# Output projection: the first head group's product stays in SBUF, and the list of steps counts transfers by size

## The chip, the cores and the metric

One Trainium2 chip, one core of it. The metric is the device time of one execution in microseconds (us); the time of a kernel is the median of its runs. A core has five engines that work at the same time, each through its own instructions in order: TensorE (PE, matrix products; PEld is its loading of weights), VectorE (DVE), ScalarE (ACT), GpSimd (POOL), and SyncE (SP), which here issues nearly all transfers between DRAM and the on-chip memory SBUF. Transfers run on 16 DMA engines. Products land in PSUM, in eight banks. An engine that waits for a semaphore holds up everything behind it in its order.

## The reference

One layer of a streaming encoder, float32, 1024 positions of 1024 features:

```
proj = rmsnorm(x) @ w_in                 # q, k, v of two head groups, and forget gates
y_fox = forgetting_attention(...)        # 8 heads of 64, causal
y_chk = chunked_relpos_attention(...)    # 8 heads of 64, a band of 9 chunks of 64
y = concat([rmsnorm(y_fox) * g_fox_out, rmsnorm(y_chk) * g_chk_out])     # 1024 x 1024
x = x + rmsnorm(y @ w_out) * g_mix_post          # the output projection
x = x + rmsnorm(memory_cross_attention(rmsnorm(x), rmsnorm(mem))) * g_mem_post
x = x + rmsnorm(square(relu(rmsnorm(x) @ w_ff1)) @ w_ff2) * g_ff_post
```

As y has two halves with an inverse root of their own per position, y @ w_out is the product of group 0 (fox) scaled by its root, plus that of group 1 (chk) scaled by its root.

## The kernel before

Every float32 product is made of three products of a rounded part (hi) and the rest (lo): `mm3` emits hi x hi (L174), lo x hi (L175) and hi x lo (L176). A weight block of 512 KB is loaded by SP (`wraw...`, L321), rounded on ACT (L338, `whi`), and its rest is formed on DVE (L343) or POOL (L346), `wlo`.

**The list of steps.** The order of the instructions of a large part of the kernel is not written out; it is made while the program is built, by a small simulation (`Flow`). Streams of PE steps each have a condition and an assumed duration; at each point of the list's own clock the first stream whose condition holds gives its next step. Other work is put into one line per engine: "V" (DVE), "S" (ACT), "G" (POOL) and "D" (transfers on SP), with an assumed cost and a level (the lower one goes first). What a step waits for is `there(key)`: the key has an assumed time, and it is past. The list decides order only; on the chip each engine waits for what it really needs. `flow.load` puts a transfer: 0.55 on line "D", then `took` until it counts as landed (4.5 unless given). Only one transfer stands on line "D" at a time.

Room is counted as tokens: `free["u4"]` for the 31 tiles of 128 x 1024 float32 that most of the layer shares (tag `u4`), `free["raw"]` for the 3 buffers of raw weight blocks, `free["mm"]` for 2 PSUM banks, `free["klo"]` for 4 tiles of attention keys, and so on.

**The stretch around the change** (phase 1 of the list, after the attention's projections; PE between about 480 and 660 us):

1. `fold_steps`: the memory keys are multiplied into w_mq, so that logits come from one product. There are two halves (k = 0, 1), each over four blocks `mq`; a block gives two banks, which ACT copies out (L944, tile `fm`). A finished tile of 512 KB is stored (`ml`, L920). When the four stores of a half have landed, POOL forms four sums (L913), which are stored too (`mlT`, L909), each after a delay of 10.0 times its number on the list's clock.
2. `mix_steps(0)`: group 0's products `yw`, in the order (th, nh) = (0,0), (0,1), (1,0), (1,1), where th is a half of the positions and nh a half of the output features, four row blocks each, 12 matrix products of 128 x 512 for each of the 16. They need `parts[th, 0]`, prepared by `Outputs`: it reads four transposed head outputs of 256 KB from DRAM (`oin` from `od`, L1072), which ACT scales and rounds (`yT_hi`, L1066) and DVE completes (`yT_lo`, L1067); ACT squares them (L1069), DVE adds the squares (`sq`, L1047), PE transposes them (`ssh`, L1096, `rstd_steps`), and DVE and POOL make the inverse root `rs`. `Outputs` goes through (th, g) = (0,0), (1,0), (0,1), (1,1), and takes seven `u4` tiles for one.
3. ACT copies a finished product, scaled by `rs`, to a tile `yt` of tag `klo` (L1233); SP stores it to DRAM (`yd`, L1235).
4. `memory_value_steps`: memory values from w_mv (`mv`).
5. `Back` loads group 0's rows from `yd` again into four `u4` tiles `yw` per half (L1206), and `mix_steps(1)` adds group 1's products to them on DVE (L1244). That is phase 2 of the list.

`Stock` loads the weight blocks ahead of use in one fixed order (mq, then wo of group 0, mv, wo of group 1, ml, mo); the dma is emitted at once, and line "D" only counts its time. wo and mv may go to a free `u4` tile when the three raw buffers are taken (`SPARE`), if 12 are free. What a split block occupies, its home, is a pair of tags `w`, `wq` or two `u4` tiles.

Of the kernel before, what the change touches and what calls it, by code (L numbers as in the profile page):

```python
# [22 lines left out]
P = 128  # L23
# [11 lines left out]
def f(ap):  # L35
    return ap.bitcast(F32)
# [19 lines left out]
class Flow:  # L56
# [15 lines left out]
        self.count += 1  # L72
        self.waiting[eng].append((level, at, self.count, cost, call, then))

    def load(self, at, call, then=None, took=4.5):
        self.put("D", at, 0.55, call, then and (lambda end: then(end + took)))

    def chain(self, at, parts, then=None, level=2):

# [56 lines left out]
def build(ctx, tc, nc, out, t):  # L136
# [65 lines left out]
    rall = const.tile([P, TB], F32, name="rall")  # L202

    od = [[dr.tile([3, P, HT], F32, name=f"od{k}_{h}") for h in range(2)] for k in range(KC)]
    yd = [dr.tile([P, D], F32, name=f"yd{b}") for b in range(TB)]
    x1d = [dr.tile([P, D], F32, name=f"x1d{b}") for b in range(TB)]
    x2d = [dr.tile([P, D], F32, name=f"x2d{b}") for b in range(TB)]
    rd = dr.tile([8, 768], F32, name="rd")
# [61 lines left out]
    class Stock:  # L270
# [3 lines left out]
        def __init__(self):  # L274
            self.blocks = []
            for n, (kind, pr) in enumerate(ORDER):
                if n == 5:
                    self.blocks.append("norm")
                b = (0 if kind == "f" else 8) + pr
                self.blocks.append((("q", n), t["w_qk"][b], [P, KC, P]))  # L280
                if n > 3:
                    self.blocks.append((("v", n), t["w_v"][n - 4], [P, KC, P]))
                if n == 7:
                    self.blocks.append("mem")
                self.blocks.append((("k", n), t["w_qk"][b + 4], [P, KC, P]))
            self.blocks += [(("mk", nb), t["w_mk"][nb], [P, KC, P]) for nb in range(KC)]
            self.blocks += [(("mq", kc), t["w_mq"][kc], [P, KC, P]) for kc in FOLD]
            pair = [P, 2, HT]
            self.blocks += [(("wo", 0, nh, i), row_pair(t["w_out"], i, nh), pair) for nh in range(2) for i in range(2)]
            self.blocks += [(("mv", nh, kp), row_pair(t["w_mv"], kp, nh), [P, 2, HT])  # L290
                            for nh in range(2) for kp in range(4)]
            self.blocks += [(("wo", 1, nh, i), row_pair(t["w_out"], 2 + i, nh), pair) for nh in range(2) for i in range(2)]
            ml = [[(("ml", 0, pr, kp), mld[pr][kp], pair) for pr in range(2) for kp in range(4)],
                  [(("ml", 1, p, k), src(k), pair) for p, (_, src) in enumerate(ML) for k in range(2)]]
            self.blocks += ml[0] + ml[1]
            self.blocks += [(("mo", 0, p, kp), src(kp), pair) for p, (_, src) in enumerate(MO) for kp in range(2)]
            self.blocks += [(("mo", 1, nh, kp), row_pair(t["w_mo"], kp, nh), pair)
                            for nh in range(2) for kp in range(4)]
            self.home = {("q", 0): "u4", ("k", 0): "u4", ("wo", 0, 1, 0): "u4", ("wo", 0, 1, 1): "u4", ("wo", 1, 1, 0): "wq", ("wo", 1, 1, 1): "u4"}
            self.home.update({(w, nb): "u4" for nb in range(1, KC, 2) for w in ("mk", "mq")})  # L300
            self.home.update({("mv", nh, kp): "u4" for nh in range(2) for kp in (1, 3)})
            self.home.update({("mo", 1, 0, kp): "wq" for kp in (1, 3)})
            turn = 0
            for b in self.blocks:
                if b[0][0] in ("ml", "mo"):
                    if b[0][:3] == ("mo", 1, 1):
                        self.home[b[0]] = "u4"
                    elif b[0][:2] == ("ml", 1) and b[0][3] == 1:
                        self.home[b[0]] = "u4"
                    elif b[0][:2] != ("mo", 1):  # L310
                        self.home[b[0]] = ("w", "wq")[turn % 2]
                        turn += 1
            self.raw, self.w, self.turned, self.spare = {}, {}, 0, {}
            self.to_load, self.to_split = list(self.blocks), []
# [50 lines left out]
        def pump(self):  # L365

            while self.to_load:
# [13 lines left out]
                    break  # L381
                free["u4" if self.spare[key] else "raw"].take()
                self.load()
                flow.put("D", flow.now, 0.55, lambda: None, lambda at, k=key: seen.__setitem__(("raw", k), at + 4.2))
            while self.to_split and there(("raw", self.to_split[0])):
                key = self.to_split[0]
                home = self.home.get(key, "w")
# [505 lines left out]
    def fold_steps(keep):  # L893
        km = keep.pop(0)
        stored, sums = all_of("folded", 8), all_of("summed_up", 8)
        for k in range(2):
            raw = {}

            def after(at, k=k, raw=raw):
                T = {"T1": (0, 0), "T3": (0, 1), "T2": (1, 1), "T4": (1, 0)}  # L900
                steps = [("T1", (0, 1), (0, 0)), ("T3", (1, 1), (0, 1)), ("T2", (1, 1), (0, 0)), ("T4", (1, 0), (1, 1))]

                def go(at, i=0):
                    if i < 4:
                        n, x, y = steps[i]
                        d = raw[T[n]]

                        def summed(end, n=n, d=d, i=i):
                            flow.load(end + 10.0 * i, lambda: nc.sync.dma_start(mlt[n][k], d),  # L909
                                      lambda e: (free["u4"].give(e), sums(e)), 3.0)  # L910
                            go(end, i + 1)

                        flow.put("G", at, 2.4, lambda: nc.gpsimd.tensor_sub(d, raw[x], raw[y]), summed, 1)  # L913

                go(at)
# [2 lines left out]

            def split(at, a, pr, k=k, raw=raw, summing=summing):
                flow.load(at, lambda: nc.sync.dma_start(mld[pr][a * 2 + k], raw[a, pr]),  # L920
                          lambda e: (stored(e), summing(e)), 3.0)

            for a in range(2):
                part = {}
# [2 lines left out]
                for j in range(2):  # L927
                    kc = a * 4 + k * 2 + j
                    for pr in range(2):
                        for h in range(2):  # L930
# [14 lines left out]
                            d, ps.rearrange("p a b -> p (a b)"), AF.Copy, scale=gm[:, kc:kc + 1]),  # L945
                            lambda at, bk=bk, one=part[pr]: (free[bk].give(at), one(at)), 1)
                    stock.done(("mq", kc))
        for _ in range(4):
            free["u4"].give(flow.end)

# [71 lines left out]
    class Outputs:  # L1022
# [5 lines left out]
        def pump(self):  # L1028
            while self.left:
                th, g = self.left[0]  # L1030
                if not (there(("od", g, th)) and ((th, g) == (0, 0) or there("keys")) and free["u4"].ready(13 if (th, g) == (0, 0) else 9)):
                    break
                self.left.pop(0)
                for _ in range(7):
# [3 lines left out]
        def one(self, th, g):  # L1038
# [19 lines left out]
            for i in range(2):  # L1058
                for j in range(2):
# [9 lines left out]
                            lambda end: (split(end), flow.put("S", end, 0.63, lambda: nc.scalar.activation(  # L1069
                                dst, o, AF.Square), squared, 1)), 1)  # L1070

                    flow.load(flow.now, lambda o=o, src=od[kc][th]: nc.sync.dma_start(o, src[0]), loaded, 5.0)  # L1072

    outputs = Outputs()
    waiting = {}
# [55 lines left out]
    class Rows:  # L1131
# [5 lines left out]
        def pump(self):  # L1137
            while self.left and free["xt"].ready() and stock.past("wo"):
# [7 lines left out]
                    xin[nm, n] = p2.tile([P, D], F32, tag="xt", bufs=2, name=f"xt{nm}{n}")  # L1146
                    nc.sync.dma_start(xin[nm, n], t["x"][n * P:(n + 1) * P, :] if nm == "w" else x1d[n])

                flow.load(flow.now, load, mark(("xt", nm, n)))

    def close_row(nm, n, at, dst, gnext, then):

# [10 lines left out]

        def store(end):
            free["xt"].give(end)
            flow.load(end, lambda: nc.sync.dma_start(dst[n], y), mark(("x1d", n)) if nm == "w" else None, 3)

            def inverse():
                c = r2[:, n:n + 1]
# [18 lines left out]
        nc.gpsimd.tensor_scalar(e, s2, EPS, EPS ** 0.5, op0=ALU.add, op1=ALU.mult)  # L1188
        nc.gpsimd.tensor_tensor(e, e, e, op=ALU.mult)

    stored = [all_of(("yd", th), 8) for th in range(2)]

    class Back:


        def __init__(self):
            self.left = [0, 1]

        def pump(self):
            while self.left and there(("yd", self.left[0])) and free["u4"].ready(6) and (  # L1200
                    there(("rs", 1, 1)) if self.left[0] else there("vm")):
                th = self.left.pop(0)
                y_tiles("w", th)
                done = all_of(("yb", th), 4)
                for b in range(4):
                    flow.load(flow.now, lambda b=b, th=th: nc.sync.dma_start(ys["w", th][0][b], yd[th * 4 + b]), done)  # L1206

    def y_half(name):
        return p1.tile([P, HT], F32R, tag="klo", bufs=4, name=name)

    def mix_steps(g):

        for th, nh in ((0, 0), (0, 1), (1, 0), (1, 1)):
            cs = slice(nh * HT, (nh + 1) * HT)
            for b in range(4):
                c = slice(b * P, (b + 1) * P)
                for k in range(4):
                    yield (0.681, lambda: k % 2 or there(("wo", g, nh, k // 2)) and (k or
                           there(("y", th, g)) and free["mm"].ready()
                           and (free["klo"].ready() if g == 0 else there(("yb", th)))))  # L1220
                    if k == 0:
                        free["mm"].take()
                        if g == 0:
                            free["klo"].take()
                        ps = mm_tile([P, HT], f"yw{th}{g}{nh}{b}")
                        yh, yl, sq = parts[th, g]
                    wh, wl = stock.w["wo", g, nh, k // 2]
                    mm3(ps, yh[k // 2][:, k % 2, c], yl[k // 2][:, k % 2, c],
                        wh[:, k % 2, :], wl[:, k % 2, :], k == 0, k == 3)
                if g == 0:  # L1230
                    yt = y_half(f"yt{th}{nh}{b}")
                    def leave(at, yt=yt, ps=ps, th=th, b=b, cs=cs):
                        flow.put("S", at, 0.63, lambda: nc.scalar.activation(  # L1233
                            f(yt), ps, AF.Copy, scale=parts["rs", th, 0][:, b:b + 1]), lambda at: (
                                free["mm"].give(at), flow.load(at, lambda: nc.sync.dma_start(yd[th * 4 + b][:, cs], f(yt)),  # L1235
                                                               lambda end: (free["klo"].give(end), stored[th](end)), 2.3)))

                    when(("rs", th, 0), flow.end, leave)
                else:
# [537 lines left out]
    def filler_steps(keep):  # L1777
# [9 lines left out]
        seen["paired"] = flow.end  # L1787
        yield from memory_key_steps(keep)
        yield from fold_steps(keep)
        seen["keys"] = flow.end  # L1790
        yield from mix_steps(0)
        yield from memory_value_steps(keep)

    def attention_phase():
# [3 lines left out]
            for th in range(2):  # L1798
                seen["v", n, th] = 0.0
        biases = Biases()  # L1800
        flow.pumps += [stock.pump, biases.pump, outputs.pump, back.pump, WeightSums().pump]
        flow.run([value_steps(), turn_steps(), score_steps(), side_steps(), rstd_steps(0), rstd_steps(1, (0,)),
                  filler_steps(keep)])
        return keep

    stock = Stock()
    back = Back()
    with tc.manual_schedule():
        nc.scalar.dma_start(gp, t["g_pre"])
        tiny = small.tile([P, 1], F32, tag="tiny", bufs=1, name="tiny")  # L1810
# [872 lines left out]
```

## Time and profile before

| what | us |
|---|---|
| median of 3 runs (1461.63 to 1462.76) | 1462.01 |
| the profiled execution | 1461.79 |
| its span, first to last instruction | 1460.0 |
| PE busy in the span | 1440.4 |
| DVE busy | 967.8 |
| ACT busy | 848.7 |
| POOL busy | 438.4 |

The kernel moves 274.13 MB, 188 GB/s over the span; the mean granted clock of TensorE was 0.997. Busy time of PE counts matrix products whose ends overlap, so 99% busy is not 99% of its peak. In rows of the profile "a<-b" is a tile written from a tile read, in the kernel's names with buffer numbers left out; `x12` is a count; what stands in square brackets behind an instruction is how long its engine had been idle, and what released it. A row of a window gives its length, the busy time of PE, PEld, DVE, ACT and POOL with their counts, the granted clock, the DMA engines' share and GB/s.

### The profile page before, as it was taken

To read this page: it belongs to the slowest core of one execution; us is meant where nothing else is said; L and a number is where in the kernel's file an instruction comes from. 1 tells how busy PE (TensorE), PEld (TensorE's weight loads), DVE (VectorE), ACT (ScalarE), POOL (GpSimd) and SP (SyncE) were. 2 spreads that over 40 slices of the span, in tenths; PEclk is the share of its full clock that TensorE was granted. 3 is DMA by queue.
4 is the path that set the end of the run, shared out by engine and by line. 5 is a ranking of instruction groups with operands and counts; after the bars stand their busy time and mean duration, and the time that the engine had idled before them with its cause. 6 is when DMAs were issued, how large, how long until landed. Compare 5 with 4: busy or idle time off the path is not lost.

```text
span 1460.0 us, 21001 instructions
## 1 busy us (share of the span) xinstructions
PE 1440.4 (99%) x7212; PEld 1216.8 (83%) x7212; DVE 967.8 (66%) x1661; ACT 848.7 (58%) x1510; POOL 438.4 (30%) x493
## 2 busy tenths in 40 slices
PE   9999999999999979999999999999999999999998
PEld 9888888888889968888788878888888888888886
DVE  5577778867677455786776587765555656655576
ACT  7457776667577745567886465545555443444442
POOL 1345555445344460252302504343322000000021
PEclk9999999999999999999999999999999999999999
DMA  8234567854546898573345557754444785445565
GB/s 333 69 98 97 143 168 185 279 125 114 130 103 189 267 326 297 204 240 102 108 152 196 188 165 244 256 199 159 159 146 164 287 318 182 136 149 196 182 251 202
DMA packets 105291, 274.13 MB, mean 188 GB/s; under 512 B 13257, under 2 KB 25809, under 8 KB 105185
## 3 DMA queue, kind: packets, MB, share of 16 engines
q1 hardware_dynamic: 100432, 264.40, 54.1%
q0 software_dynamic: 4608, 8.39, 3.8%
q8 instruction: 57, 0.93, 0.3%
q14 instruction: 50, 0.40, 0.1%
q10 hardware_dynamic: 144, 0.00, 0.0%
HBM read 188.28 MB, written 84.47 MB: 187 GB/s over the span
## 4 chain that ended last, share of the span: by engine, by line
PE 91%; DVE 3%; DMA 3%; ACT 2%; issue 1%; POOL 0%; DVEq 0%; POOLq 0%; SPq 0%; ACTq 0%
PE pv L654 4%; PE fx L175 4%; PE fx L176 4%; PE fx L174 4%; PE ptr L604 4%; PE fy L175 3%; PE fy L176 3%; PE fy L174 3%; PE px L176 3%; PE px L174 3%; PE px L175 3%; PE k L174 2%; PE k L176 2%; PE k L175 2%; PE q L174 2%; PE pz L174 2%
## 5 line engine op out<-in xcount | busy, mean ns | idle before, releaser
L610 DVE TENSOR_TENSOR p<-ptr,p 128x512 fp32r<-128x512 f32 (+1 forms) x152 | 92.3, 616 | 31.6 <-ACT p L613 30.4
L2405 ACT ACTIVATE whif<-ra 128x1024 fp32r<-128x1024 f32 x37 | 39.3, 1061 | 127.0 <-PE fy L175 62.6
L2519 POOL TENSOR_SCALAR rf<-sf,e 128x1 f32<-128x1 f32 x8 | 8.5, 1068 | 324.2 <-ACT jf L2504 324.2
L2407 DVE TENSOR_TENSOR wlof<-ra,whif 128x1024 fp32r<-128x1024 f32 x37 | 45.3, 1225 | 89.4 <-ACT whif L2405 89.4
L613 ACT ACTIVATE p<-ptr 128x512 fp32r<-128x512 f32 (+1 forms) x152 | 79.6, 538 | 42.7 <-PE ptr L604 41.9
L654 PE MATMUL pv<-p,vs 128*128 128x512 f32 (+1 forms) x304 | 86.2, 371 | 0.4 <-DVE p L610 0.4
L176 PE MATMUL fx<-vhif,wlof 128*128 128x512 f32 x168 | 65.4, 389 | 0.0
L174 PE MATMUL fx<-vhif,whif 128*128 128x512 f32 x168 | 65.4, 389 | 0.0
L175 PE MATMUL fx<-vlof,whif 128*128 128x512 f32 x168 | 65.4, 389 | 0.0
L2294 POOL TENSOR_TENSOR sc<-wf,wf 128x512 f32<-128x512 f32 x14 | 22.2, 1583 | 141.9 <-DMA wf<-in_w_ff 116.0
L654 PEld LDWEIGHTS pv<-p,vs 128*128 128x128 f32 x304 | 53.1, 189 | 8.8 <-DVE p L610 0.8
L174 PE MATMUL yw<-whiwo,yT_hi 128*128 128x512 f32 x128 | 51.2, 400 | 5.5 <-ACT yt L1233 5.5
L174 PE MATMUL k<-hT_hi,whik 128*128 128x512 f32 x128 | 52.6, 411 | 0.0
L175 PE MATMUL yw<-wlowo,yT_hi 128*128 128x512 f32 x128 | 50.7, 396 | 1.0 <-DVE wlowo L343 1.0
L174 PE MATMUL q<-hT_hi,whiq 128*128 128x512 f32 x128 | 51.0, 399 | 0.0
L176 PE MATMUL yw<-whiwo,yT_lo 128*128 128x512 f32 x128 | 50.5, 395 | 0.0
L176 PE MATMUL k<-hT_hi,wlok 128*128 128x512 f32 x128 | 50.2, 392 | 0.0
L175 PE MATMUL k<-hT_lo,whik 128*128 128x512 f32 x128 | 50.2, 392 | 0.0
L175 PE MATMUL q<-hT_lo,whiq 128*128 128x512 f32 x128 | 50.1, 391 | 0.0
L176 PE MATMUL q<-hT_hi,wloq 128*128 128x512 f32 x128 | 50.0, 391 | 0.0
L174 PE MATMUL fy<-vhif,whif 128*128 128x512 f32 x128 | 49.8, 389 | 0.0
L175 PE MATMUL fy<-vlof,whif 128*128 128x512 f32 x128 | 49.8, 389 | 0.0
(747 smaller groups left out, 5013.2 us busy)
## 6 DMA issues: line engine op xcount, KB each, us to landing
ra<-gd SPq DMA_DIRECT2D x56, 512.0 KB, 3.5
wg<-in_w_ff SPq DMA_DIRECT2D x56, 512.0 KB, 4.9
wf<-in_w_ff SPq DMA_DIRECT2D x38, 512.0 KB, 4.0
gd<-s SPq DMA_DIRECT2D x48, 256.0 KB, 2.1
od<-ot SPq DMA_DIRECT2D x64, 128.0 KB, 2.5
od<-od POOLq DMA_DIRECT2D x32, 256.0 KB, 5.3
gd<-u SPq DMA_DIRECT2D x32, 256.0 KB, 2.1
wrawml<-ml SPq DMA_DIRECT2D x14, 512.0 KB, 4.4
```

The costliest lines, as they stand in the source:

```text
L174: nc.tensor.matmul(ps, lh, rh, start=start, stop=False, skip_group_check=more)
L175: nc.tensor.matmul(ps, lh, rl, start=False, stop=False, skip_group_check=more)
L176: nc.tensor.matmul(ps, ll, rh, start=False, stop=stop, skip_group_check=more)
L604: nc.tensor.transpose(tr[:, m, :], sp[:, k * P:(k + 1) * P], ident)
L610: flow.put("V", at, 0.56 if dead else 0.7, lambda: nc.vector.tensor_sub(pl[:, live, :], tr[:, live, :], f(ph[:, live, :])), done)
L613: flow.put("S", flow.end, 0.49 if dead else 0.6, lambda ph=ph, tr=tr, live=live: nc.scalar.activation(ph[:, live, :], tr[:, live, :], AF.C ...
L654: nc.tensor.matmul(pv[:, :, q0 * P:(q0 + k1 - k0) * P], v, x[:, :, k0:k1, :].rearrange("p m k q -> p m (k q)"), start=c == 0 and m == 0, s ...
L2294: eng.tensor_sub(sc[:, k1], r0[:, k0], r1[:, k0])
L2405: nc.scalar.activation(ah, ra, AF.Copy)
L2407: nc.vector.tensor_sub(al, ra, f(ah))
L2519: nc.gpsimd.tensor_scalar(r, ssf[b][:, 0:1], ssf[b][:, 1:2], e3[:, b:b + 1], op0=ALU.add, op1=ALU.add)
```

## The change

Group 0's copies go straight into the row tiles `yw`, which are taken from `u4` when a half's first product begins; `yd`, `Back` and the `klo` tiles `yt` are gone, and group 1's products wait for the copy of their row (`y0`). On the list, line "D" counts 1.4 for a transfer of 512 KB of the kinds mq, wo, mv, ml, mo, mlT, xt and x1d, 0.75 for a read of 256 KB in `Outputs`, and what is left until a landing is shorter to match. The key "keys", which lets `Outputs` go on to (1,0), is set after the first half of the fold, where it was set after both; `Outputs` needs 8 free tiles, before 9. The four sums' stores are delayed by 4.0 times their number. One mv block, (1, 2), has its home in `u4`.

```diff
-    def load(self, at, call, then=None, took=4.5):
-        self.put("D", at, 0.55, call, then and (lambda end: then(end + took)))
+    def load(self, at, call, then=None, took=4.5, cost=0.55):
+        self.put("D", at, cost, call, then and (lambda end: then(end + took)))
...
-    yd = [dr.tile([P, D], F32, name=f"yd{b}") for b in range(TB)]
...
             self.home.update({("mo", 1, 0, kp): "wq" for kp in (1, 3)})
+            self.home.update({("mv", 1, 2): "u4"})
...
                 self.load()
-                flow.put("D", flow.now, 0.55, lambda: None, lambda at, k=key: seen.__setitem__(("raw", k), at + 4.2))
+                big = key[0] in ("mq", "wo", "mv", "ml", "mo")
+                flow.put("D", flow.now, 1.4 if big else 0.55, lambda: None,
+                         lambda at, k=key, big=big: seen.__setitem__(("raw", k), at + (3.4 if big else 4.2)))
...
-                            flow.load(end + 10.0 * i, lambda: nc.sync.dma_start(mlt[n][k], d),
-                                      lambda e: (free["u4"].give(e), sums(e)), 3.0)
+                            flow.load(end + 4.0 * i, lambda: nc.sync.dma_start(mlt[n][k], d),
+                                      lambda e: (free["u4"].give(e), sums(e)), 2.5, 1.4)
...
                 flow.load(at, lambda: nc.sync.dma_start(mld[pr][a * 2 + k], raw[a, pr]),
-                          lambda e: (stored(e), summing(e)), 3.0)
+                          lambda e: (stored(e), summing(e)), 2.5, 1.4)
...
                     stock.done(("mq", kc))
+            seen.setdefault("keys", flow.end)          # fold_steps, after a half
...
-  ... and free["u4"].ready(13 if (th, g) == (0, 0) else 9)):
+  ... and free["u4"].ready(13 if (th, g) == (0, 0) else 8)):
...
-                    flow.load(flow.now, lambda o=o, src=od[kc][th]: nc.sync.dma_start(o, src[0]), loaded, 5.0)
+                    flow.load(flow.now, lambda o=o, src=od[kc][th]: nc.sync.dma_start(o, src[0]), loaded, 5.0, 0.75)
...
-                flow.load(flow.now, load, mark(("xt", nm, n)))
+                flow.load(flow.now, load, mark(("xt", nm, n)), 4.0, 1.4)
...
-            flow.load(end, lambda: nc.sync.dma_start(dst[n], y), mark(("x1d", n)) if nm == "w" else None, 3)
+            flow.load(end, lambda: nc.sync.dma_start(dst[n], y), mark(("x1d", n)) if nm == "w" else None, 3, 1.4)
...
-    class Back: ...                                    # y_tiles("w", th), 4 loads from yd
-    def y_half(name): ...                              # a tile of tag klo
...
-                           and (free["klo"].ready() if g == 0 else there(("yb", th)))))
+                           and (g or ("w", th) in ys or free["u4"].ready(4))
+                           and (g == 0 or there(("y0", th, nh, b)))))
                     if k == 0:
                         free["mm"].take()
-                        if g == 0:
-                            free["klo"].take()
+                        if g == 0 and ("w", th) not in ys:
+                            y_tiles("w", th)
...
                 if g == 0:
-                    yt = y_half(f"yt{th}{nh}{b}")
-                    def leave(at, yt=yt, ps=ps, th=th, b=b, cs=cs):
+                    def leave(at, yc=ys["w", th][0][b][:, cs], ps=ps, th=th, b=b, nh=nh):
                         flow.put("S", at, 0.63, lambda: nc.scalar.activation(
-                            f(yt), ps, AF.Copy, scale=parts["rs", th, 0][:, b:b + 1]), lambda at: (
-                                free["mm"].give(at), flow.load(at, lambda: nc.sync.dma_start(yd[th * 4 + b][:, cs], f(yt)),
-                                                               lambda end: (free["klo"].give(end), stored[th](end)), 2.3)))
+                            yc, ps, AF.Copy, scale=parts["rs", th, 0][:, b:b + 1]),
+                            lambda at: (free["mm"].give(at), mark(("y0", th, nh, b))(at)))
...
         yield from fold_steps(keep)
-        seen["keys"] = flow.end
         yield from mix_steps(0)
```

More of the change, by code (lines that the diff above doesn't have):

```diff
@@ L1030, in pump @@
                 th, g = self.left[0]
-                if not (there(("od", g, th)) and ((th, g) == (0, 0) or there("keys")) and free["u4"].ready(13 if (th, g) == (0, 0) else 9)):
+                if not (there(("od", g, th)) and ((th, g) == (0, 0) or there("keys")) and free["u4"].ready(13 if (th, g) == (0, 0) else 8)):
                     break
@@ L1189, in guard @@
         nc.gpsimd.tensor_tensor(e, e, e, op=ALU.mult)
[L1191 to L1209, printed above, removed]
     def mix_steps(g):
@@ L1800, in attention_phase @@
         biases = Biases()
-        flow.pumps += [stock.pump, biases.pump, outputs.pump, back.pump, WeightSums().pump]
+        flow.pumps += [stock.pump, biases.pump, outputs.pump, WeightSums().pump]
         flow.run([value_steps(), turn_steps(), score_steps(), side_steps(), rstd_steps(0), rstd_steps(1, (0,)),
@@ L1806, in build @@
     stock = Stock()
-    back = Back()
     with tc.manual_schedule():
```

## The prediction

> **What bounds the kernel now.** I read the page's head and chain first: they say which engine decides.
>
> ```profile
> span 1460.0 us, 21001 instructions
> PE 1440.4 (99%) x7212; PEld 1216.8 (83%) x7212; DVE 967.8 (66%) x1661; ACT 848.7 (58%) x1510; POOL 438.4 (30%) x493
> PE 91%; DVE 3%; DMA 3%; ACT 2%; issue 1%; POOL 0%; DVEq 0%; POOLq 0%; SPq 0%; ACTq 0%
> ```
>
> TensorE (PE) holds 91% of the chain, and the change removes no matmul. So it can win only where PE waits. Next: who made PE wait between 480 and 660 us, where the projection's two head groups run (waiter, line, releaser: us, times, longest).
>
> ```profile
> PE yw L174 <- ACT yt L1233: 5.5, 1, 5.5
> PE ssh L1096 <- DVE sq L1047: 1.2, 1, 1.2
> PE yw L175 <- DVE wlowo L343: 1.0, 1, 1.0
> ```
>
> Three waits, 7.7 us, all in group 0's product. To see what they cost beyond themselves, the windows (span, busy time per engine, clock, DMA share, GB/s):
>
> ```profile
> 510.00:522.00 12.00, 10.96 (x51) 8.83 (x50) 9.90 (x3) 3.85 (x5) 11.84 (x5) 1.00 1.03 383
> 528.40:530.00 1.60, 1.59 (x4) 1.30 (x5) 0.92 (x2) 1.60 (x3) 0.21 (x1) 0.50 1.05 417
> 530.00:532.00 2.00, 2.00 (x7) 1.52 (x6) 1.87 (x1) 1.71 (x4) 2.00 (x1) 0.50 1.03 412
> 532.00:534.00 2.00, 2.00 (x9) 1.63 (x8) 2.00 (x2) 1.23 (x2) 1.92 (x2) 0.92 0.58 230
> 538.00:560.00 22.00, 22.00 (x101) 18.17 (x100) 11.99 (x17) 15.63 (x25) 3.26 (x4) 1.00 0.71 258
> 560.00:590.00 30.00, 30.00 (x136) 24.86 (x135) 15.41 (x16) 14.19 (x18) 1.20 (x2) 1.00 0.82 291
> ```
>
> After the 5.5 us wait the granted clock is 0.50 for 3.6 us and 0.92 for two: 1.60 x 0.5 + 2.00 x 0.5 + 2.00 x 0.08 = 2.0 us more. So this place costs 7.7 + 2.0 = **9.7 us**. The DMA engines are full (share 1.03 to 1.05) from 510 to 532, and from 538 to 590 PE has no gap at all.
>
> Why the copy was late: ScalarE (ACT) in order of time.
>
> ```profile
> 514.75 0.69 ACT L1233 ACTIVATE yt<-yw,rs 128x512 f32<-128x512 f32 x1 [2.28 <-PE yw L176]
> 517.47 0.69 ACT L1233 ACTIVATE yt<-yw,rs 128x512 f32<-128x512 f32 x1 [2.04 <-PE yw L176]
> 526.40 1.38 ACT L1066 ACTIVATE yT_hi<-oin,gcol 128x512 fp32r<-128x512 f32 x2 [8.24 <-DMA oin<-od]
> 527.69 0.67 ACT L1233 ACTIVATE yt<-yw,rs 128x512 f32<-128x512 f32 x1
> ```
>
> The third copy stands behind two yT_hi, and these stood 8.24 us for a DMA. One product takes 517.47 - 514.75 = 2.72 us. The DMA, on the chain and in the order in which SP issued (start, time, engine, line, transfer):
>
> ```profile
> 514.37 12.01 DMA oin<-od
> 532.72 2.83 DVE sq L1047
> 537.18 0.66 PE ssh L1096 x4
> ...
> 501.40 1.55 SPq L920 DMA_DIRECT2D ml<-fm  x2
> 503.92 1.85 SPq L321 DMA_DIRECT2D wrawmv<-in_w_mv  x2
> 506.71 0.41 SPq L920 DMA_DIRECT2D ml<-fm  x1
> 507.97 0.44 SPq L321 DMA_DIRECT2D wrawmv<-in_w_mv  x1
> 508.51 0.67 SPq L920 DMA_DIRECT2D ml<-fm  x1
> 512.16 0.33 SPq L909 DMA_DIRECT2D mlT<-fm  x1
> 512.58 0.40 SPq L920 DMA_DIRECT2D ml<-fm  x1
> 513.07 0.91 SPq L321 DMA_DIRECT2D wrawmv<-in_w_mv  x2
> 514.37 5.52 SPq L1072 DMA_DIRECT2D oin<-od  x4
> ```
>
> The first read of group 0's second half needs 12.01 us, queued behind a full DMA.
>
> **The change part by part.**
>
> *No way through DRAM.* Gone are 16 stores and 8 loads:
>
> ```profile
> yd<-yt SPq DMA_DIRECT2D x16, 256.0 KB, 2.9
> yw<-yd SPq DMA_DIRECT2D x8, 512.0 KB, 6.9
> ```
>
> That is 8 MB, on SP from 522 to 594, where PE (538 to 590) waits for nothing: 0 us. If PE did wait there, it would be for mv or wo weights, which then land sooner: no loss. The 16 copies stay, with another destination: 0.
>
> *Eight of 31 tiles are held for the rows*, four from the first product on, four from the ninth. Where the products and the loads' uses stand, and a load's time:
>
> ```profile
> L174 PE MATMUL yw<-whiwo,yT_hi x128: 388/389/794, 510.5 to 634.0; 128*128 128x512 f32 x128
> L174 PE MATMUL mv<-whimv,mT_hi x32: 389/389/389, 565.9 to 586.9; 128*128 128x512 f32 x32
> wrawmv<-in_w_mv SPq DMA_DIRECT2D x8, 512.0 KB, 9.5
> L944 ACT ACTIVATE fm<-fm,gm x16: 677/688/690, 486.5 to 510.8; 128x512 f32<-128x512 f32 x16
> ```
>
> Spare loads need 12 free tiles, so the two mv loads at 513.07 will wait for an ordinary buffer. What hides that is the distance to their use, the second half of the memory values: (565.9 + 586.9) / 2 = 576.4, 63 us after their issue. If that cover is gone: one load, 2.9 us as yd's where the DMA is not full, 9.5 where it mostly is, and 1.2 for its low half (row of 1225 ns below): 4.1 to 10.7. Taken as 0, as no gap is there now; bounds 0 and 10.7. ("mv",1,2) as u4 only moves a split's home, and a store's release sooner (4.0 for 10.0) only frees tiles: 0, or a part of that price.
>
> *"keys" after the first half of the fold.* The 16 fold copies run from 486.5 to 510.8, so half are done about 499 and the reads of (1,0) can be asked for some 11 us sooner. By my count over the code's takes and gives 10 tiles are free then; 8 are needed.
>
> *Sizes.* From the mq loads on, 512 KB counts 1.4 on the list's one DMA line, a read 0.75. That is about this stretch's speed: 512 KB at 383 GB/s is 1.37 us. Asked at 499, the reads queue behind loads asked before, but ahead of: the second ml at 501.40, ml at 506.71, 508.51 and 512.58, mlT at 512.16, and two mv at 513.07. Seven transfers, 7 x 1.37 = 9.6 us. So the first read lands at 526.4 - 9.6 = **516.8**. Bounds: 514.4 (its present issue) and 522.3 (three of seven passed). I take 516.8, as all seven are asked later in the code.
>
> *What is late next.* On ACT the reads' yT_hi will also be listed earlier: I expect two ahead of the **first** copy. It then ends at 516.8 + 1.38 + 0.67 = 518.8. PE has two banks; with mixing begun at 510.5 it wants the first bank back at 510.5 + 2 x 2.72 = 515.9. Wait: **2.9 us**. The wlowo wait (1.0) came from the split of a wo block on VectorE (DVE), slowed while GpSimd (POOL) formed the sums:
>
> ```profile
> L913 POOL TENSOR_TENSOR fm<-fm,fm 128x1024 f32<-128x1024 f32 x8 | 21.8, 2733 | 3.2 <-DMA yd<-yt 2.9
> L343 DVE TENSOR_TENSOR wlowo<-wrawwo,whiwo 128x1024 fp32r<-128x1024 f32 x3 | 10.5, 3534 | 4.5 <-ACT whiwo L338 4.5
> L2407 DVE TENSOR_TENSOR wlof<-ra,whif 128x1024 fp32r<-128x1024 f32 x37 | 45.3, 1225 | 89.4 <-ACT whif L2405 89.4
> ```
>
> 3534 ns against 1225 for the same shape elsewhere. The sums wait for the fourth ml store, which now follows the reads, so they start after 518; the wait goes. Should it stay, it is contained in the 2.9.
>
> The ssh transpose needs sq. Now: 537.18 - 526.40 = 10.8 us after the first read landed, with one yT_lo (2.58) and one sq (2.83) held. The normal values:
>
> ```profile
> L1067 DVE SCALAR_TENSOR_TENSOR yT_lo<-oin,gcol,yT_hi x16: 741/751/2583, 335.2 to 554.6; 128x512 fp32r<-128x512 f32 x16
> L1047 DVE TENSOR_TENSOR sq<-sq,oin x12: 671/692/2893, 345.0 to 557.5; 128x512 f32<-128x512 f32 x12
> ```
>
> Without holding: 10.8 - (2.58 - 0.75) - (2.83 - 0.69) = 6.8. So sq is ready at 523.6 to 527.6. PE comes to ssh after about four products and the wait: 510.5 + 10.9 + 2.9 = 524.3. Wait 0 to 3.3; I take 1.6, since the sums still run then but hold few operations.
>
> *Clock.* Waits of 1.0 and 1.2 us left the clock at 1.00, 5.5 us did not. A wait of 2.9 lies between: 0 to 2.0 us. I take 0, nearest to 1.2. The Trainium skill, "TensorE: Matmul & The Clock Gate", Part 1, puts the limit at an idle window of about 3.4 us, free-running: by it also 0 here, though 0.5 us more of waiting would cross it; half the clock after the long wait agrees with it.
>
> **The sum.** 9.7 goes, 2.9 + 1.6 = 4.5 comes: **5.2 us less**. The profiled execution took 1461.79 us (span 1460.0, 1.8 around it): 1456.6. The median of the runs is 0.2 above it: **1456.8**.
>
> **The rivals.**
>
> *B: the wait goes entirely.* If reads land by 514, or the copies stay ahead of yT_hi on ACT, at most 1 of the 9.7 us stays: 1462.0 - 9.2 = 1452.8. For it: the list's new costs match the measured 1.37 us, so ACT's order may fit the landings. Against: the DMA stays full.
>
> *C: the tiles run short.* The held rows delay reads of group 1 or weights, and PE waits for one of them between 538 and 590. For it: mv loads lose their early start. Against: no gap there now, and 8 MB less traffic. Of the 0 to 10.7 us take 4.1, the DMA not being full there: 1456.8 + 4.1 = 1460.9.
>
> *D: the reads are listed earlier than they land (slower).* The copy wait is L - 513.9 for a first landing at L, because it is now the first copy that stands behind them, not the third. With three of seven passed, L = 522.3: wait 8.4, clock 2.0, ssh 1.6, together 12.0 against 9.7: 1464.3. It decides from L = 520.0 on (6.1 + 2.0 + 1.6 = 9.7).
>
> *E: POOL's sums hold every DVE step.* All four yT_lo at 2.58 and three adds at 2.89 in a row from 518.8: 19.0, so sq at 537.8, ssh waits 13.5, clock 2.0, copy 2.9: 18.4, 8.7 more than now: 1470.7. The rows speak against: one of four and one of three were held with POOL busy. The Trainium skill, "SBUF — State Buffer", "SBUF: two separate sides", has a lock for the whole instruction between GpSimd and a DVE operation with two SBUF inputs; 3534 against 1225 ns agrees, but not every operation met it.
>
> **How the numbers follow.** Forecast (A) 0.42, own range 1454 to 1460 (ends of ssh, clock and landing); B 0.28; C 0.16; D 0.10; E 0.04. The 8-in-10 range leaves out E, half of D and the lower edge of B: 1451.5 to 1463. About 0.2% (2.9 us) is what a measurement of this kernel can tell from no change. Faster, below 1459.1: A 0.37, B 0.28, C 0.03: 0.68. Same: A 0.05, C 0.10, D 0.02: 0.17. Slower: 0.15.
>
> **What would show it.** The chain's "DMA oin" piece near 514 goes or shrinks from 12; the oin reads are issued before 510; PE's row for the copy (then "yw") falls from 5.5 to about 3, ssh stays 0 to 3; clock 1.00 between 510 and 540; no yd rows; 538 to 590 without a gap. The prediction is wrong if the reads still follow the seven transfers, if ACT takes copies first (B), or if PE waits for mv, wo or group 1's yT in mixing.

## The result, and the profile after

| kernel | median, us | runs from to | ratio to the kernel before, 95% interval |
|---|---|---|---|
| before | 1461.82 | 1460.15 to 1462.76 | |
| changed | 1453.5 | 1453.31 to 1453.93 | 0.9945 [0.9928, 0.9962] |

The change makes the kernel 8.3 us faster. The forecast was 5.2 us less, 1456.8. The measured time lies in the wide range of the prediction (1451.5 to 1463), but below the own range of its forecast A (1454 to 1460), and 0.7 us from rival B's 1452.8.

The head and the chain of the changed kernel's page:

```profile
span 1451.9 us, 20939 instructions
PE 1437.6 (99%) x7212; PEld 1214.9 (84%) x7212; DVE 960.0 (66%) x1661; ACT 848.8 (58%) x1510; POOL 437.3 (30%) x493
PE 90%; DVE 3%; DMA 3%; ACT 2%; POOL 1%; issue 1%; DVEq 0%; POOLq 0%; SPq 0%; ACTq 0%
```

PE still has nine tenths of the chain. Who made PE wait between 480 and 660 us (waiter, releaser: us, times, longest):

```profile
PE ssh L1099 <- DVE sq L1050: 1.1, 1, 1.1
```

The waits for the copy (5.5) and for wlowo (1.0) are gone, and ssh waits 1.1 where it waited 1.2. The windows of the changed kernel (length, busy time per engine, clock, DMA share, GB/s):

```profile
510.00:522.00 12.00, 11.93 (x61) 9.86 (x60) 9.43 (x8) 9.41 (x14) 3.25 (x2) 1.00 1.05 386
528.00:530.00 2.00, 2.00 (x11) 1.65 (x10) 0.00 (x0) 0.50 (x1) 1.92 (x2) 1.00 1.00 282
530.00:532.00 2.00, 2.00 (x11) 1.65 (x10) 0.00 (x0) 0.69 (x1) 1.82 (x3) 1.00 1.03 414
538.00:560.00 22.00, 22.00 (x100) 18.20 (x100) 10.14 (x12) 13.64 (x20) 6.33 (x4) 1.00 0.59 207
```

The clock is 1.00 throughout, so the place that cost 9.7 us now costs 1.1: 8.6 us less, against 8.1 us less span (small waits elsewhere differ by under 1 us each). From the first matmul of the mixing (`yw`) to the first of the next phase (`ms`) PE takes 115.5 us, before 124.2: the gain lies here. Two of the small waits, 0.7 and 0.8 us longer than before, lie ahead of the place, so the mixing begins at 511.82 in this trace and at 510.46 in the trace before. Moments of two traces are best compared counted from there. Four engines in order of time, of the changed kernel (start, time, instruction, idle before and releaser):

```profile
508.09 5.66 SPq L1075 DMA_DIRECT2D oin<-od  x4
513.80 3.62 SPq L922 DMA_DIRECT2D ml<-fm  x5
517.72 0.33 SPq L228 DMA_DIRECT2D g_mix_post<-in_g_mix_post  x1
518.36 0.97 SPq L1150 DMA_DIRECT2D xtw<-in_x  x2
...
514.77 0.69 ACT L1217 ACTIVATE yw<-yw,rs 128x512 f32<-128x512 f32 x1 [0.17 <-PE yw L176]
517.06 2.03 ACT L1069 ACTIVATE yT_hi<-oin,gcol 128x512 fp32r<-128x512 f32 x3 [1.60 <-DMA oin<-od]
519.52 0.67 ACT L1217 ACTIVATE yw<-yw,rs 128x512 f32<-128x512 f32 x1
...
513.69 5.06 DVE L343 TENSOR_TENSOR wlowo<-wrawwo,whiwo 128x1024 fp32r<-128x1024 f32 x2 [1.65 <-ACT whiwo L338]
514.98 2.68 POOL L915 TENSOR_TENSOR fm<-fm,fm 128x1024 f32<-128x1024 f32 x1
518.68 2.91 DVE L1070 SCALAR_TENSOR_TENSOR yT_lo<-oin,gcol,yT_hi 128x512 fp32r<-128x512 f32 x4
522.58 0.82 POOL L629 DMA_DIRECT2D od<-od  x1 [4.92 <-DMA od<-od]
523.15 7.95 POOL L915 TENSOR_TENSOR fm<-fm,fm 128x1024 f32<-128x1024 f32 x3
523.52 2.85 DVE L1050 TENSOR_TENSOR sq<-sq,oin 128x512 f32<-128x512 f32 x1 [0.54 <-ACT oin L1072]
```

What to see. The reads are issued at 508.09 (before: 514.37) and the first lands at 517.06 (526.40), that is 5.2 us after the mixing began (15.9). **One** copy stands ahead of the first yT_hi (before: two). By the time it lands, PE is in its second product. The copy at 519.52, behind three yT_hi and a square, is just in time. POOL idles from 517.66 to 522.58, for a DMA; in that gap the four yT_lo take 0.73 us each. Then the sums go on, and the last square add takes 2.85 us: that is the 1.1 us of ssh. SP's queue shows something that the prediction had not foreseen: g_mix_post and two loads xtw, 512 KB each, are issued here, some 52 us earlier than before, since without the `yt` tiles the memory for them comes free earlier (s_held below shows it).

### The profile page after: what moved, and what is told of

The parts are those of the page before. It is cut to its first block, busy times and chain, and to the rows that moved or that the text cites. A ratio compares the mean times of both kernels' runs of the same rounds, so it can differ in the third digit from the quotient of the medians.

```text
span 1451.9 us, 20939 instructions
## 1 busy us (share of the span) xinstructions
PE 1437.6 (99%) x7212; PEld 1214.9 (84%) x7212; DVE 960.0 (66%) x1661; ACT 848.8 (58%) x1510; POOL 437.3 (30%) x493
## 4 chain that ended last, share of the span: by engine, by line
PE 90%; DVE 3%; DMA 3%; ACT 2%; POOL 1%; issue 1%; DVEq 0%; POOLq 0%; SPq 0%; ACTq 0%
PE pv L656 4%; PE fx L175 4%; PE fx L176 4%; PE fx L174 4%; PE ptr L606 4%; PE fy L175 3%; PE fy L176 3%; PE fy L174 3%; PE px L176 3%; PE px L175 3%; PE px L174 3%; PE q L174 2%; PE q L175 2%; PE q L176 2%; PE pz L174 2%; PE pz L175 2%
```

## The experiments

**Parts of the change.** Three parts: S, the rows in SBUF; C, the sizes on the list; K, the earlier key and the eight tiles. The change has two small parts besides, the spacing of 4.0 between the sums' stores and the home of mv (1, 2). The kernels with two parts and the changed one have them, those with one part don't, and no run tries them alone.

| kernel | parts | median, us | ratio to before, 95% interval |
|---|---|---|---|
| s_only | S | 1463.5 | 1.0016 [1.0007, 1.0025] |
| sizes_only | C | 1463.78 | 1.0024 [1.0014, 1.0034] |
| keys_only | K | 1466.36 | 1.0041 [1.0026, 1.0056] |
| no_early | S, C | 1458.16 | 0.9981 [0.9972, 0.9991] |
| no_sizes | S, K | 1468.76 | 1.0051 [1.0034, 1.0068] |
| no_sbuf | C, K | 1458.27 | 0.9980 [0.9971, 0.9989] |
| changed | S, C, K | 1453.5 | 0.9945 [0.9928, 0.9962] |

The kernel before ran beside them at medians of 1460.4 to 1461.8 us. Each part alone makes the kernel slower; the three together make it 0.55% faster. Nothing here adds up part by part. As the small parts come in with the pairs, a share of the step from one part to two may be theirs.

*s_only*: the kernel before with the changed `mix_steps` and without `yd` and `Back`.

```diff
-                    yt = y_half(f"yt{th}{nh}{b}")
+                    def leave(at, yc=ys["w", th][0][b][:, cs], ...   # and y_tiles at the first product
```

> Only the rows kept in SBUF; the list's old costs, the old place of keys, 9 free tiles, the spacing 10.0. Theory 1 (what counts is where ACT's order has the yT_hi of (1,0) against the landing of their reads): the third copy stands behind three yT_hi and a square, and the reads behind the same stores as before, with two mv loads less but three loads of 512 KB more (g_mix_post and two xtw, which may now start in phase 1) ahead of them: landing about 527.8 us, PE waits about 8 us for the third copy, with the low clock 2 more: 1461 to 1466 us. Theory 2 (8 MB less traffic is what made it faster): 1453 to 1456.

Measured 1463.5 us (1462.64 to 1466.35). The waits between 480 and 660 us:

```profile
PE yw L174 <- ACT yw L1213: 7.8, 1, 7.8
PE yw L175 <- DVE wlowo L342: 1.3, 1, 1.3
```

SP in order of time:

```profile
509.09 0.47 SPq L228 DMA_DIRECT2D g_mix_post<-in_g_mix_post  x1
509.96 1.35 SPq L1146 DMA_DIRECT2D xtw<-in_x  x2
516.30 4.74 SPq L1071 DMA_DIRECT2D oin<-od  x4
```

The three early loads stand ahead of the reads, these are issued at 516.30, and the copy's wait grows from 5.5 to 7.8. The 8.4 MB that are no longer moved show as no gain.

*s_held*: is it these loads? s_only, with four unused tiles allocated through phase 1, which keep that memory taken.

```diff
+        for i in range(4):
+            nc.gpsimd.memset(p1.tile([P, S], F32, tag="klo", bufs=4, name=f"hold{i}")[:, 0:1], 0.0)
```

> Only the rows in SBUF (as s_only), but four unused tiles of the halves' size stay allocated through phase 1, so that the memory for the three 512 KB loads (g_mix_post and two of xtw) comes free no earlier than in the kernel before. Theory 1 (s_only lost because these three loads, 52 us early, stood ahead of the first reads of od on SyncE's queue): the loads are issued at about 570 again, the first oin is issued about 4 us earlier than in s_only (512 instead of 516.3) and lands at about 523.5, the wait for the copy falls from 7.8 to about 3.7 us, and the time is 1457.5 to 1459.5 us. Theory 2 (the rows in SBUF cost by themselves): the time stays at 1462.5 to 1464.5 us.

Measured 1460.25 us (1459.16 to 1463.27), 0.9996 [0.9986, 1.0005]. PE's wait for the copy:

```profile
PE yw L174 <- ACT yw L1213: 5.5, 2, 4.5
```

SP in order of time:

```profile
515.06 0.33 SPq L908 DMA_DIRECT2D mlT<-fm  x1
515.99 3.19 SPq L1071 DMA_DIRECT2D oin<-od  x4
```

The loads are gone from the stretch. This trace is of the longest of the ten runs, and its mixing begins 2.2 us later than that of s_only (512.55 against 510.31). Counted from there, the first read is issued 2.6 us earlier than in s_only (3.4 us after it, against 6.0), now behind an mlT store, and lands 4.9 us earlier (12.4 against 17.3). The wait shrinks to 4.5, and in the median the loss of s_only is gone. So the direction held, and my 512 for the issue was too early. The rows in SBUF by themselves are worth nothing that can be measured.

*stores_back*: is it the traffic? The changed kernel, storing the held halves as well.

```diff
-                            lambda at: (free["mm"].give(at), mark(("y0", th, nh, b))(at)))
+                            lambda at: (free["mm"].give(at), mark(("y0", th, nh, b))(at),
+                                flow.load(at, lambda: nc.sync.dma_start(yd[th * 4 + b][:, cs], yc), None, 2.3)))
```

> The changed kernel, which in addition stores each of the sixteen held halves to DRAM (16 x 256 KB = 4.2 MB, half of the traffic that the change removes) and never reads them; the order of all other work up to the first of these stores is the same. Theory 1 (the traffic that goes is worth nothing, the prediction's term of 0): the time is 1453.0 to 1454.3 us, and the waits are those of the changed kernel. Theory 2 (part of the gain is the traffic): the second four reads of od and the mlT stores queue behind the new stores on SyncE's queue, a wait for yT_hi or sq of over 1 us appears behind 540, and the time is 1455 to 1458 us.

Measured 1452.84 us (1452.38 to 1453.42), 0.9946 [0.9929, 0.9962]: the changed kernel's time. Its one wait there of over 0.5 us is 1.6 us, at the same ssh. The 16 stores, half of the traffic that the change removes, are free; the eight loads alone weren't put back.

*no_sizes*: the changed kernel with the old costs on line "D".

```diff
-                big = key[0] in ("mq", "wo", "mv", "ml", "mo")
-                flow.put("D", flow.now, 1.4 if big else 0.55, ...
+                flow.put("D", flow.now, 0.55, ...     # and 0.55 for ml, mlT, xt, x1d and the reads
```

> The changed kernel with the list's old costs for transfers (0.55 for all). Theory 1: the list expects the reads of (1,0) far too early and puts four yT_hi ahead of the last four fold copies on ACT; first landing about 513 us, the fold's copies are held from about 506, PE waits 5 to 6 us in the fold and runs 4 us at the low clock: 1459 to 1462 us. Theories 2 and 3: 1453 to 1455, since traffic and early reads are there.

Measured 1468.76 us (1468.26 to 1468.91). Waits:

```profile
PE fm L174 <- ACT fm L944: 5.0, 1, 5.0
PE ssh L1097 <- DVE sq L1048: 4.4, 1, 4.4
PE yw L175 <- DVE wlowo L343: 2.1, 1, 2.1
```

The list believes the reads to land early and puts yT_hi ahead of the last fold copies; ACT stands, PE stands behind it. The mechanism was foreseen, the two other waits were not, and the time is 6.8 us above the range. *keys_only*, the kernel before with

```diff
+            seen.setdefault("keys", flow.end)   # and 8 for 9 tiles
```

> The kernel before, with only the earlier keys and the eight tiles. The list puts the first yT_hi ahead of six of the fold copies and ssh after 5 matmuls of the product. Theory 1 (as in no_sizes, ACT then waits for the landing while fold copies stand behind it): TensorE waits 4 to 6 us for fm and 3 to 6 us for sq, the clock falls to 0.6 to 0.8, and the time is 1466 to 1471 us. Theory 2 (the reads are issued earlier and so nothing is lost): the time is 1458 to 1462 us.

gives the same picture at 1466.36 us (1465.91 to 1468.09): 5.1 for fm, 4.5 for ssh, 2.0 for wlowo, as theory 1 had it (four fold copies stand behind the first yT_hi, not six).

*no_early*: the changed kernel with "keys" set after both halves, and nine tiles.

```diff
-            seen.setdefault("keys", flow.end)
+        seen["keys"] = flow.end            # behind fold_steps
```

> The changed kernel with keys set after both halves of the fold and 9 tiles asked, so that the reads of (1,0) are issued after all stores of the fold. Theory 1: with the new costs the list expects them late, and puts five copies ahead of the first yT_hi on ACT; landing about 529 us, the sixth copy due at 528: PE waits 1 to 3 us for it, no low clock: 1453.5 to 1457 us. Theory 3 (the early reads are what made it faster): the long wait is back, 1460 to 1463.

Measured 1458.16 us (1456.47 to 1460.46). The first read is issued at 518.54 and each wait is short; PE's three waiting matmuls, in order of time:

```profile
532.87 0.50 PE L174 MATMUL yw<-whiwo,yT_hi 128*128 128x512 f32 x1 [2.29 <-ACT yw L1216]
539.00 0.50 PE L176 MATMUL yw<-whiwo,yT_lo 128*128 128x512 f32 x1 [1.06 <-DVE yT_lo L1069]
540.90 0.50 PE L174 MATMUL yw<-whiwo,yT_hi 128*128 128x512 f32 x1 [0.70 <-ACT yw L1216]
```

Windows around them (the clock is the third column from the end):

```profile
536.00:538.00 2.00, 1.94 (x8) 1.23 (x7) 2.00 (x2) 0.63 (x1) 2.00 (x1) 1.00 1.01 372
542.00:544.00 2.00, 2.00 (x8) 1.76 (x8) 0.69 (x1) 0.00 (x0) 0.19 (x1) 0.50 0.51 207
```

Five copies stand ahead of yT_hi, as expected, and the late landing costs less than in the kernel before. But the three waits are 4.1 us together, where 1 to 3 were expected, and behind the third the clock is 0.50: 0.12 x 2 + 0.50 x 2 + 0.23 x 2 = 1.7 us more (0.88, 0.50 and 0.77 in the windows from 540 to 546). Both put the time above the range of theory 1, and below that of theory 3.

*no_sbuf*: the changed kernel with `yt`, `yd` and `Back` as before (the reverse of the diff of s_only).

> All of the change but the rows in SBUF: group 0's product still goes through DRAM (yd and back), with the new costs, the early keys, the spacing 4.0 and the mv home. Theory 1: ACT's order is that of the changed kernel (one copy, three yT_hi), the first read lands near 517, PE's wait for the copy is gone: 1453 to 1455.5 us. Theory 2: most of the gain is lost, 1459 or more.

Measured 1458.27 us (1457.4 to 1460.74): outside both theories. Waits:

```profile
PE ssh L1100 <- DVE sq L1051: 4.4, 2, 3.1
PE yw L174 <- ACT yt L1237: 1.1, 1, 1.1
```

The copy's wait is down to 1.1 without S, as theory 1 said. What I had not seen: the list puts ssh nine matmuls earlier on PE than in the changed kernel, and it waits 3.1 us there and 1.3 at the next; behind the 3.1 the clock falls to 0.50 (528 to 530 us).

*sizes_only*: the kernel before with the costs of line "D" alone (the reverse of the diff of no_sizes).

> The kernel before, with only the list's transfer sizes of the change (rows still through DRAM, keys as before). The list now puts four copies ahead of the first yT_hi on ACT (two in the kernel before). Theory 1 (the gain is the place of the copies on ACT against the landing of the reads): the wait for the copy (5.5 us) falls to 1.5 us or less, ssh stands after 80 matmuls and waits 0 to 2 us, the clock stays at 1.00; the time is 1455 to 1458.5 us. Theory 2 (without the rows in SBUF the sizes bring nothing: the fifth half tile waits for the first store to land, or the reads come later still): a wait of 3 us or more in place of the old one, and the time is 1459.5 to 1463 us.

Measured 1463.78 us (1462.96 to 1465.14). Theory 1's order came, four copies ahead of yT_hi, and the time did not; it is 0.8 us above theory 2's range, and for another reason than theory 2's. Its waits:

```profile
PE yw L174 <- ACT yt L1235: 4.9, 1, 4.9
PE ssh L1098 <- DVE sq L1049: 3.6, 1, 3.6
```

POOL and DVE in order of time:

```profile
521.61 16.54 POOL L915 TENSOR_TENSOR fm<-fm,fm 128x1024 f32<-128x1024 f32 x6
522.77 10.39 DVE L1069 SCALAR_TENSOR_TENSOR yT_lo<-oin,gcol,yT_hi 128x512 fp32r<-128x512 f32 x4 [9.18 <-ACT yT_hi L1068]
533.09 6.40 DVE L1049 TENSOR_TENSOR sq<-sq,oin 128x512 f32<-128x512 f32 x3
```

POOL's sums run without a gap, 2.76 us each, and every yT_lo beside them takes 2.60 us (0.73 in the changed kernel). ACT's squares wait for each yT_lo, and the fifth copy stands behind the squares. This is rival E's mechanism, in a kernel where it does happen.

**POOL's sums.** *late_sums*: the changed kernel, with the sums 18 us later on the list.

```diff
-                        flow.put("G", at, 2.4, lambda: nc.gpsimd.tensor_sub(d, raw[x], raw[y]), summed, 1)
+                        flow.put("G", at + (18.0 if i == 0 else 0.0), 2.4, ...
```

> The changed kernel, but POOL's sums of the fold halves stand 18 us later on the list, behind the part of the mix in which DVE makes yT_lo and the square sums. Theory 1 (POOL's sums hold DVE's operations of two SBUF inputs): the four yT_lo take 0.7 us each and none of the square sums over 1 us, sq is ready 2 to 3 us earlier and the first ssh wait (1.1 us) is gone; the two wlowo between 513.7 and 518.7 take 1.2 us each. The time is 1452.0 to 1453.6 us, unless the later mlT costs something behind it. Theory 2 (DVE is slow there for another reason, the DMA traffic for one): yT_lo and sq keep their times (one square sum of about 2.8 us), and the ssh wait stays at 0.9 to 1.4 us.

Measured 1455.28 us (1454.35 to 1457.54), 0.9964 [0.9951, 0.9977]. DVE in order of time, and the matmul whose wait lost time again:

```profile
511.77 2.36 DVE L343 TENSOR_TENSOR wlowo<-wrawwo,whiwo 128x1024 fp32r<-128x1024 f32 x2 [1.65 <-ACT whiwo L338]
521.70 0.69 DVE L1050 TENSOR_TENSOR sq<-sq,oin 128x512 f32<-128x512 f32 x1 [0.54 <-ACT oin L1072]
...
585.44 1.09 PE L1099 MATMUL ssh<-ident,sq 128*128 128x128 f32 x4 [3.13 <-DVE sq L1050]
```

The window behind that wait:

```profile
586.00:588.00 2.00, 2.00 (x7) 1.65 (x6) 1.43 (x2) 0.00 (x0) 0.66 (x1) 0.50 0.02 4
```

Without the sums beside them, two wlowo take 2.36 us (5.06 in the changed kernel) and the last square add 0.69 (2.85); the first ssh waits for nothing. Theory 1 of the holding is shown. The time is lost again not at the next ssh but at the third of the stretch, that of group 1's second half. The second four reads are issued at 551.93 (535.87 in the changed kernel), behind six mlT stores and two mv loads, and the third four only from 569.85 to 575.22 (from 556.38): ssh waits 3.13 us and the clock falls to 0.50. *late_sums_12*, 12.0 in place of 18.0, keeps those reads where the change has them.

> As late_sums, but POOL's sums stand 12 us later on the list instead of 18, so that the second four reads of od come ahead of the last four mlT stores on SyncE's queue, as in the changed kernel. Theory 1 (POOL's sums were what held the last square sum, and the 3.1 us that late_sums lost at the second ssh came from the late second reads): both ssh waits are gone, the clock stays at 1.00 in 500 to 600, and the time is 1450.5 to 1452.5 us, under the changed kernel (1453.5). Theory 2 (the later sums hold the second yT_lo and square sums instead): the first ssh waits 0, the second 2 to 4 us, and the time is 1454 to 1456.5 us.

Measured 1452.73 us (1451.51 to 1454.06), 0.9945 [0.9931, 0.9958]: as the changed kernel. The first ssh waits for nothing, the second 0.2, no clock falls, but the second copy comes 0.9 us late: here the first read lands 6.0 us after the mixing began, in the changed kernel 5.2. So the last 1.1 us can be moved and not, here, be measured as a gain.

**The copy's place on ACT.** *reads_3us*: the changed kernel, the list assuming that a read lands after 3.0 us; this was to give the order that I had predicted, two yT_hi ahead of the first copy.

```diff
-  ... loaded, 5.0, 0.75)
+  ... loaded, 3.0, 0.75)
```

> The changed kernel, but the list assumes that a read of od lands 3.0 us after its issue (5.0 in the change). The list then puts two yT_hi ahead of the first copy, and whiwo_1_1 behind the copies. This is the order that the prediction assumed for the change. Theory 1 (the copy's place on ACT against the landing of the first read decides): the read still lands at about 517.0, two yT_hi and the copy end at about 519.1, where TensorE wants the bank at 517.4, so the third product waits 1.5 to 2.9 us for the copy; wlowo_1_1 now stands behind two of the square sums on DVE, which may add 0.5 to 2 us; the time is 1455.5 to 1458.5 us, that is 2 to 5 us over the changed kernel. Theory 2 (the gain comes from the traffic that goes, the order matters little): within 1 us of the changed kernel, 1452.5 to 1454.5 us, with no wait of over 1 us for the copy.

Measured 1466.01 us (1463.8 to 1468.12), 1.0034 [1.0021, 1.0047]. ACT's first copy with what stands ahead of it, PE's two waiting matmuls and a row of DVE:

```profile
517.64 2.03 ACT L1069 ACTIVATE yT_hi<-oin,gcol 128x512 fp32r<-128x512 f32 x3 [3.11 <-DMA oin<-od]
519.58 0.67 ACT L1217 ACTIVATE yw<-yw,rs 128x512 f32<-128x512 f32 x1
...
520.30 0.50 PE L174 MATMUL yw<-whiwo,yT_hi 128*128 128x512 f32 x1 [1.97 <-ACT yw L1217]
...
535.02 1.22 DVE L343 TENSOR_TENSOR wlowo<-wrawwo,whiwo 128x1024 fp32r<-128x1024 f32 x1 [11.30 <-DMA mlT<-fm]
536.90 1.11 PE L1099 MATMUL ssh<-ident,sq 128*128 128x128 f32 x4 [7.90 <-DVE sq L1050]
```

A window behind the first wait:

```profile
522.00:524.00 2.00, 2.00 (x6) 1.52 (x6) 1.32 (x2) 2.00 (x4) 0.99 (x2) 0.50 1.02 418
```

Three yT_hi stand ahead of the first copy, not the two that I expected here and in the prediction, and PE waits 1.97 us for it. One yT_hi less, (519.58 - 517.64) / 3 = 0.65 us, would leave about 1.3; this is an estimate. So a copy behind yT_hi does hold PE. The rest of the loss is another thing: the last wlowo got a tile out of which an mlT store was still reading. The list takes such a store to be done 2.5 us after its turn; it landed at 534.9, 12.6 us after its issue. DVE stood 11.3 us before wlowo, the last square add behind it.

*reads_8us*: the same line with 8.0; two copies ahead of yT_hi, ssh 12 matmuls later.

> The changed kernel, but the list assumes that a read of od lands 8.0 us after its issue (5.0 in the change; the trace of the changed kernel shows 8.9 for the first). The list then puts two copies ahead of the first yT_hi, and ssh 12 matmuls later on TensorE. Theory 1: the copies are as early as before, the ssh wait of 1.1 us goes, and the time is 1452.0 to 1453.5 us, 0 to 1.2 us under the changed kernel. Theory 2 (yT_hi behind one copy more moves sq by as much as ssh moves): the ssh wait stays at 0.7 to 1.5 us and the time is 1453 to 1454.5 us.

Measured 1465.52 us (1464.69 to 1467.27), 1.0031 [1.0019, 1.0043]; neither theory. ACT:

```profile
531.40 0.69 ACT L1217 ACTIVATE yw<-yw,rs 128x512 f32<-128x512 f32 x1 [9.25 <-DMA mlT<-fm]
```

Here a held row tile itself got such memory: the third copy stood 9.25 us for the mlT store, and PE 7.6 for the copy. That these tiles' memory is the cause rests on the releaser in these two rows; a kernel with the same order and other memory wasn't tried.

## Why the prediction was right, and where it was off

- *The 9.7 us that go*: right. 7.7 us of waits and 2.0 of slow clock were there, and 1.1 us is left.
- *The reads' landing*: 516.8 predicted, 517.06 measured, but in a trace whose mixing begins 1.4 us later. From the mixing's start it is 6.3 predicted and 5.2 measured. Six transfers were overtaken, not seven (four ml, an mlT, one mv). At 1.37 us each that is 8.2 us, but counted from the mixing's start the reads came 15.9 - 5.2 = 10.7 us earlier. What moved them by the rest stays open, and that the two moments nearly agree is luck.
- *"I expect two ahead of the first copy"*: the step that failed. The changed list put one copy ahead of yT_hi, and the term of 2.9 measured 0. It was too large for the predicted order too, as the reads land earlier: with the rows of the changed kernel, 517.06 + 1.38 + 0.67 - (511.82 + 2 x 2.72) = 1.9. No run made the predicted order; with three yT_hi ahead (reads_3us) the copy waits 1.97 us.
- *ssh*: 1.6 taken, 1.1 measured; sq is ready 9.3 us after the landing, within the 6.8 to 10.8. That POOL's sums make the difference is shown by late_sums, where it is 7.1 (522.39 - 515.25).
- *wlowo*: the wait went, and for the reason given, though the time given for it is wrong. Before, POOL's first sum started at 509.44, and the split that PE waited for took 3.77 us beside it. Now the first sum starts at 514.98, not behind 518, and this split ran ahead of it, in 1.22 us. Of the two in the row of 5.06 us only the second is held still (3.92), and PE doesn't wait for it.
- *Traffic 0*: right as far as tried (half of it in stores_back, all of it in s_held). *Held tiles 0*: right for this kernel. The price of rival C was right in size, 0 to 10.7, but its place was not: not a late weight, but a tile whose former content was still being stored (7.6 and 7.9 us of PE).
- *Clock 0*: right, as no wait over 1.1 us came. The reason was weak: in reads_3us it fell to 0.50 behind a wait of 1.97 us, so with the 2.9 us it could well have fallen.

The terms give 2.9 + 0.5 = 3.4 us too much, the forecast was 3.3 us too high. By the prediction's own sign ("if ACT takes copies first (B)") its path A is not what happened: rival B's is, for the first copy, and the second is just in time behind three yT_hi. The time lies in the range because the range held B; D's and E's mechanisms are real and appear in reads_3us, no_sizes and sizes_only, on orders that the change avoids.

That the sizes themselves make the gain is not shown: they pay only with one of the other parts (and the two small ones), and why the list then comes out as it does was read from its orders, not proved.

## What to carry to other kernels

In an order planned by hand or by a list, one instruction that waits for a transfer holds everything behind it on its engine: write down which instructions stand ahead of the wait, in the order after the change, before pricing it. Parts of a change to a planned order are not additive, so test the whole and each part. A planner's assumed landing must fit the queue at that place (9 to 13 us here, 2.5 to 5 assumed), also where it only hands out memory: bringing one of them alone nearer to the measured one, the reads' from 5.0 to 8.0, made the kernel about 12 us slower.

## What the runs showed of the hardware

- The clock fell after shorter waits than expected: to 0.50 after a wait of 1.97 us (reads_3us), after 3.09 (no_sbuf) and 3.13 (late_sums), and after 2.29, 1.06 and 0.70 within 10.3 us (no_early), where the 2.29 alone had left it at 1.00. The waits of 1.0 to 1.6 us at this place in the kernel before, the changed one and stores_back did not lower it. The Trainium skill, "TensorE: Matmul & The Clock Gate", Part 1, has the array go cold after at least one idle window of about 3.4 us, free-running. That the same length acts at one place and not at another agrees with free-running; that 1.97 us was enough does not agree with a wholly idle window.
- DVE beside POOL: with POOL's sums back to back (2.65 to 2.76 us each), each DVE operation with two SBUF inputs takes about one sum's time (2.60 for 0.73 in sizes_only, 2.58 in s_held). The Trainium skill, "SBUF — State Buffer", "SBUF: two separate sides", calls this an exclusive lock for the whole instruction; the rows of sizes_only agree. In the kernel before, three of the four yT_lo ran unheld while POOL stood still, from 526.90 to 529.79, and the fourth, beside the next sum, took 2.58.
- With the DMA share at 1.03 to 1.05, a transfer of 256 or 512 KB took 7 to 13 us from issue to landing, and 2.6 us at the least where less was under way (an mlT store of the changed kernel).
